# Recurrence of an RWKV-7 layer: the running sum of the log decay taken of the raw hyperbolic tangent, split in two halves

## The chip, the cores and the metric

The program runs on one core of a Trainium2 chip. The time is the device time of one execution in microseconds; the kernel before takes 2631.36 us, the median of 3 runs that lie between 2630.79 and 2633.34. TensorE does the matmuls (its weight loads are a row of their own in the profile, PEld), VectorE (DVE) and ScalarE (ACT) work on tiles, GpSimd (POOL) does a few small powers, and SyncE (SP) issues most of the DMAs. Each engine takes its instructions in order.

## The reference

The model has two layers over 256 tokens of width 2048. The first mixes tokens by RWKV-7 (32 heads of 64), the second by forgetting attention; a SwiGLU of width 5632 follows each. The change touches the decay of the RWKV-7 layer and, in passing, three small loads of the attention layer:

```python
w_log = -jax.nn.softplus(-(w0 + jnp.tanh(xw @ w1) @ w2).astype(f32)) - 0.5
decay = jnp.exp(-jnp.exp(w_log))
...
S = (S * w_t[:, :, None, :] + sa[..., None] * b_t[:, :, None, :]
     + v_t[..., None] * k_t[:, :, None, :])
```

With z for the argument of the softplus turned around, `-exp(w_log)` is `-exp(-0.5) * sigmoid(z)`, and the sigmoid is `0.5 + 0.5 * tanh(z / 2)`. So the log of the decay is `NEG_HALF_EXP * (tanh(z / 2) + 1)`, with `NEG_HALF_EXP` = -0.5 exp(-0.5).

## The kernel before

All large products run in one stream of weights (class `Stream`). Blocks of 128x512 weights come from memory as float32 and are split: ScalarE copies the block to a rounded half `wh` (L149), VectorE subtracts to get the rest `wl` (L150). Every product is then three matmuls in the fast 32-bit type, xh·wh, xh·wl and xl·wh (L175 to L177), for each of two halves of the tokens. The weights are split up to six blocks ahead of TensorE, into seven buffers.

Everything else is woven into that stream. Background work is written as generators; after each group of three stream matmuls `tick` moves every active generator to its next `yield`. So the order of the work is set by where the `yield`s stand, and then by the order in which the build lays the instructions on each engine. PSUM has four banks for the stream (`mm`) and four for the background (`bg`, taken by `take` and returned by `give`).

The recurrence of the RWKV-7 layer is computed in chunks of 64 tokens, woven into the products `r`, `w2`, `a2`, `g2` and the output projection. It has eight units: four groups g of eight heads by two halves t of the tokens. For each unit `prepare` does the following.

- It has `tw`, the log decay, 128 tokens by 512 channels, computed in the foreground after the product `w2`: a tanh on ScalarE (L938), then VectorE multiplies by and adds `NEG_HALF_EXP` (L939).
- TensorE sums `tw` over the tokens of each chunk: one float32 matmul with the triangular constant (L563) into bank `ps`. Four small ones of two columns (L565) put the sum over a whole chunk into `pc`.
- VectorE takes `ps` minus `tw` (L577); ScalarE takes exponentials of `ps`, of its negative, and of the chunk sums (L578, L579, L582), later of the difference (L591).
- Transposes (L627, L641) and copies (L635, L646) bring the scaled keys to the other layout, 16 float32 matmuls (L657) form the small matrices, and VectorE reads them out of PSUM under a mask (L660).

`solve` and `merge` invert the triangular blocks (32x32 matmuls on L734, L741, L751, L767), and `chain` carries the state from chunk to chunk (L812, L815, L821, L826, L828). `post` finishes the outputs (L859, L874, transposes on L888). A unit's matmuls on L563 and L565 are issued while the unit before is in its L657 and L767.

At the start of the attention layer the kernel loads three small vectors (`bf`, and `gains` in four pieces of 64x1) by DMAs issued on GpSimd (L1038 to L1042); VectorE scales `gains` (L1043). ScalarE issues the two DMAs of `cb` there (L1051), in between its copies of weights and the statistics of the residual (`jk`, L283).

Of the kernel before, what the change touches and what calls it, by code (L numbers as in the profile page):

```python
# [8 lines left out]
F32 = mybir.dt.float32  # L9
F32R = mybir.dt.float32r  # L10
BF16 = mybir.dt.bfloat16
AF = mybir.ActivationFunctionType
ALU = mybir.AluOpType
# [4 lines left out]
P = 128  # L18
# [4 lines left out]
N = 64  # L23
C = 64
# [4 lines left out]
NEG_HALF_EXP = -0.5 * 0.6065306597126334  # L29
# [1 line left out]
MASKED = -1.0e30  # L31
POW = 6

C_ID, C_TRI, C_IND, C_M, C_E, C_B8, C_LANE, C_I8, C_CAUSAL, C_END = 0, 128, 256, 258, 386, 450, 482, 486, 550, 678

# [4 lines left out]
def constants():  # L42
    import numpy as np

    c = np.zeros((P, C_END), np.float32)
    s = np.arange(P)
    c[:, C_ID : C_ID + P] = np.eye(P)
    c[:, C_TRI : C_TRI + P] = (s[:, None] <= s[None, :]) & (s[:, None] // C == s[None, :] // C)
    c[:, C_IND] = s < C
    c[:, C_IND + 1] = s >= C  # L50
    t = np.arange(C)
    c[:, C_M : C_M + C] = (s[:, None] % C) <= t[None, :]
    c[:, C_M + C : C_M + 2 * C] = (s[:, None] % C) < t[None, :]
    a, b = s[:, None] % 32, np.arange(32)[None, :]
    for i, m in enumerate((8, 16)):
        e = (a // (2 * m) == b // (2 * m)) & (a % (2 * m) < m) & (b % (2 * m) >= m)
        c[:, C_E + 32 * i : C_E + 32 * (i + 1)] = e
    c[:, C_B8 : C_B8 + 32] = a // 8 == b // 8
    c[:, C_LANE : C_LANE + 4] = s[:, None] % 4 == np.arange(4)[None, :]
    c[:, C_I8 : C_I8 + 64] = np.eye(8).reshape(1, 64)  # L60
    c[:, C_CAUSAL : C_CAUSAL + P] = np.where(s[None, :] <= s[:, None], 0.0, MASKED)
    return c


# [135 lines left out]
def hybrid_kernel(ctx, tc, const, x, a_norm_g, a_mix, a_w_rkv, a_w0, a_w1, a_w2, a_a0, a_a1, a_a2,  # L200
                  a_g1, a_g2, a_k_k, a_k_a, a_r_k, a_lnx_g, a_lnx_b, a_w_o, b_norm_g, b_w_in, b_b_f,
                  b_qn_g, b_kn_g, b_on_g, b_w_o, f_norm_g, f_w_gu, f_w_d, final_g, out):
    nc = tc.nc
# [34 lines left out]
    mm = nc.tensor.matmul  # L238
# [12 lines left out]
    cst = small.tile([P, C_END], F32, name="cst")  # L251
# [76 lines left out]
    with ExitStack() as actx:  # L328
# [5 lines left out]
        with ExitStack() as bctx:  # L334
# [166 lines left out]
            ps = S.gemm("k0", lhs_of(xk), ready=lambda kt: has("xk", kt))  # L501
# [14 lines left out]
            for g in range(4):  # L516
                ps = S.gemm(f"v{g}", lhs_of(xv), ready=lambda kt: has("xv", kt))
# [6 lines left out]
        with ExitStack() as bctx:  # L524
            g1 = bctx.enter_context(tc.tile_pool(name="sg", bufs=1))
# [8 lines left out]
            yF = {}  # L534
            vec, wat, rts, gts, units = {}, {}, {}, {}, {}

            def bc(v, g, name):
                t_ = g1.tile([P, 512], F32, name=name)
                nc.sync.dma_start(t_[:, :], v[g * 512 : (g + 1) * 512].partition_broadcast(P))
                return t_  # L540
# [6 lines left out]
            half = [slice(0, C), slice(C, P)]  # L547
# [6 lines left out]
            def prepare():  # L554
                for i, (g, t) in enumerate(order):
                    yield from wait(("r", g))
                    tw, ta = wat[g][0][t], wat[g][1][t]
                    vk, va, vr = vec[g][:3]
                    k = K[g][:, t, :]
                    r = rts[g][t]  # L560
                    ps = yield from S.take()
                    pc = yield from S.take()
                    mm(ps[:, :], cst[:, C_TRI : C_TRI + P], tw[:, :], start=True, stop=True)  # L563
                    for p in range(4):
                        mm(pc[:, 2 * p : 2 * p + 2], tw[:, p * P : (p + 1) * P], cst[:, C_IND : C_IND + 2], start=True, stop=True)  # L565
                    kk = u1.tile([P, 512], F32, name="kk")
# [7 lines left out]
                    W, Wp = WW[:, 0, :], WW[:, 1, :]  # L574
                    Wi = u1.tile([P, 512], F32, name="Wi")
                    wc = u3.tile([P, 8], F32, name="wc")
                    nc.vector.tensor_tensor(Wp, ps[:, :], tw[:, :], op=ALU.subtract)  # L577
                    nc.scalar.activation(W, ps[:, :], AF.Exp)  # L578
                    nc.scalar.activation(Wi[:, :], ps[:, :], AF.Exp, scale=-1.0)  # L579
                    for c in range(2):  # L580
                        for q in range(2):
                            nc.scalar.activation(wc[half[c], q:8:2], pc[half[q], c:8:2], AF.Exp)  # L582
                    S.give(2)
                    n8 = u1.tile([P, 8], F32, name="n8")
                    nc.vector.tensor_reduce(n8[:, :], h4(sq[:, :]), AX.X, ALU.add)
# [2 lines left out]
                    yield  # L588
                    yield
                    yield  # L590
                    nc.scalar.activation(Wp, Wp, AF.Exp)  # L591
                    k2 = u1.tile([P, 512], F32, name="k2")
                    nc.vector.scalar_tensor_tensor(k2[:, :], ta[:, :], -1.0, va[:, :], op0=ALU.add, op1=ALU.mult)
                    nc.vector.scalar_tensor_tensor(k2[:, :], k2[:, :], 1.0, k, op0=ALU.add, op1=ALU.mult)
# [328 lines left out]
            for g in range(4):  # L923
                ps = S.gemm(f"r{g}", lhs_of(xr), ready=lambda kt: has("xr", kt))
# [10 lines left out]
                tw = []  # L935
                for t in range(2):
                    a = g1.tile([P, 512], F32, name=f"tw{t}")
                    nc.scalar.activation(a[:, :], ps[t][:, :], AF.Tanh, scale=0.5)  # L938
                    nc.vector.tensor_scalar(a[:, :], a[:, :], NEG_HALF_EXP, NEG_HALF_EXP, op0=ALU.mult, op1=ALU.add)  # L939
                    tw.append(a)  # L940
                ps = S.gemm(f"a2{g}", lambda kt: tuple(loraw["a"]))
                ta = []
                for t in range(2):
# [85 lines left out]
    with ExitStack() as bctx:  # L1029
# [5 lines left out]
        alpha = b1.tile([P, 2, 2 * H], F32, name="alpha")  # L1035
        cq = b1.tile([P, 2, H], F32, name="cq")
        bf = b1.tile([H, 1], F32, name="bf")
        nc.gpsimd.dma_start(bf[:, :], b_b_f[0][:, None])  # L1038
        gains = b1.tile([P, 2], F32, name="gains")
        for j in range(2):  # L1040
            nc.gpsimd.dma_start(gains[j * N : j * N + N, 0:1], b_qn_g[0][:, None])
            nc.gpsimd.dma_start(gains[j * N : j * N + N, 1:2], b_kn_g[0][:, None])  # L1042
        nc.vector.tensor_scalar(gains[:, 0:1], gains[:, 0:1], N ** -0.5, None, op0=ALU.mult)  # L1043
        nc.vector.tensor_scalar(rsh[:, :], rst[:, :], 0.5, None, op0=ALU.mult)

# [324 lines left out]
```

## Time and profile before

| | |
|---|---|
| median of 3 runs | 2631.36 us |
| the profiled execution | 2630.58 us, span 2628.8 us |
| TensorE busy | 2580.2 us, 98% of the span |
| weight loads busy | 2113.8 us, 80% |
| VectorE, ScalarE busy | 1674.7 us (64%), 1481.5 us (56%) |
| mean granted clock of TensorE | 0.994 |

The profile page gives each engine's busy time, the span in 40 slices, and the chain of work that ended last. Other views used below: the waits (who waited for whom, and for how long in total, how often, and the longest), a table of stretches of the span with the busy time of each engine and the granted clock of TensorE, the timeline of single instructions (start, duration, engine, line, what it writes and reads, and in brackets the idle time before it and what ended it), and the groups of instructions by line. The units of the recurrence run from about 254 to 620 us; the attention layer begins at about 1378 us. A float32 matmul shows as two records in the timeline (x2 for one L563, x8 for four L565).

### The profile page before, as it was taken

What the parts mean: (1) busy time and instruction counts of PE and PEld (TensorE: products, weight loads), DVE (VectorE), ACT (ScalarE), POOL (GpSimd) and SP (SyncE); (2) the same over time, 40 slices, a digit from 0 to 9 for tenths busy, and PEclk for the clock granted to TensorE, in tenths of its full rate; (3) what the DMA queues carried; (4) which work ended last, traced back from release to release, by engine and by line L of the source; (5) the groups of instructions that cost most, each with busy time, mean ns of one, the idle gap of its engine ahead of it and who ended that gap; (6) DMA issues with size and microseconds to landing.
All of it is one profiled execution on the core that took longest, in us unless ns stands there. A gap on an engine that the chain in (4) does not pass through costs nothing.

```text
span 2628.8 us, 40943 instructions
## 1 busy us (share of the span) xinstructions
PE 2580.2 (98%) x15160; PEld 2113.8 (80%) x15160; DVE 1674.7 (64%) x2965; ACT 1481.5 (56%) x2869; POOL 90.0 (3%) x68
## 2 busy tenths in 40 slices
PE   7999999999999999999999999999999999999998
PEld 5788777777888888888888888888888888888886
DVE  7875887777555555555556677676755555555554
ACT  6665687776545454544455556655654545454443
POOL 0000010100000000000001010010000000000000
PEclk9999999899999999999999999999999999999999
DMA  6676323235666666655556666664566666665564
GB/s 199 184 215 208 104 87 111 88 111 156 189 190 190 187 192 185 192 192 192 190 188 203 200 201 186 184 206 153 178 191 190 189 189 191 186 192 192 197 196 153
DMA packets 253946, 468.46 MB, mean 178 GB/s; under 512 B 22249, under 2 KB 32697, under 8 KB 253745
## 3 DMA queue, kind: packets, MB, share of 16 engines
q1 hardware_dynamic: 250736, 463.62, 58.2%
q8 instruction: 119, 1.95, 0.3%
q10 hardware_dynamic: 2848, 2.22, 0.3%
q14 instruction: 83, 0.67, 0.1%
q0 software_dynamic: 160, 0.00, 0.0%
HBM read 457.37 MB, written 4.23 MB: 176 GB/s over the span
## 4 chain that ended last, share of the span: by engine, by line
PE 90%; ACT 4%; DVE 3%; DMA 1%; issue 1%; POOL 0%; SPq 0%; ACTq 0%; POOLq 0%; DVEq 0%
PE mm L175 27%; PE mm L177 27%; PE mm L176 27%; DVE wl L150 2%; ACT wh L149 1%; PE bg L989 1%; PE bg L821 1%; PE bg L657 1%; PE bg L812 1%; ACT xb L635 1%; ACT Bs L859 1%; PE bg L828 1%; PE bg L815 1%; PE bg L304 1%; DMA st<-in_a_w_rkv_dram 1%
## 5 line engine op out<-in xcount | busy, mean ns | idle before, releaser
L150 DVE TENSOR_TENSOR wl<-st,wh 128x512 fp32r<-128x512 f32 (+1 forms) x1648 | 1129.4, 690 | 812.8 <-ACT wh L149 807.4
L149 ACT CAST wh<-st 128x512 fp32r<-128x512 f32 (+1 forms) x1648 | 1015.5, 622 | 946.8 <-DVE wl L150 691.9
L175 PE MATMUL mm<-wh,xb 128*128 128x512 f32 x2048 | 803.4, 392 | 0.0
L177 PE MATMUL mm<-wh,xb 128*128 128x512 f32 x2048 | 799.8, 391 | 0.0
L176 PE MATMUL mm<-wl,xb 128*128 128x512 f32 x2048 | 799.4, 390 | 0.0
L175 PEld LDWEIGHTS mm<-wh,xb 128*128 128x128 f32 x2048 | 384.7, 188 | 79.8 <-issue 3.3
L177 PEld LDWEIGHTS mm<-wh,xb 128*128 128x128 f32 x2048 | 384.5, 188 | 79.1
L176 PEld LDWEIGHTS mm<-wl,xb 128*128 128x128 f32 x2048 | 384.8, 188 | 76.0
L176 PE MATMUL mm<-wl,xa 128*128 128x512 f32 x768 | 306.0, 398 | 3.0 <-DVE wl L150 1.6
L175 PE MATMUL mm<-wh,xa 128*128 128x512 f32 x768 | 306.9, 400 | 0.0
L177 PE MATMUL mm<-wh,xa 128*128 128x512 f32 x768 | 305.4, 398 | 0.0
L175 PE MATMUL mm<-wh,hb 128*128 128x512 f32 x448 | 174.3, 389 | 0.0
L176 PE MATMUL mm<-wl,hb 128*128 128x512 f32 x448 | 174.3, 389 | 0.0
L177 PE MATMUL mm<-wh,hb 128*128 128x512 f32 x448 | 174.3, 389 | 0.0
L176 PEld LDWEIGHTS mm<-wl,xa 128*128 128x128 f32 x768 | 145.8, 190 | 33.2 <-DVE wl L150 3.3
L177 PEld LDWEIGHTS mm<-wh,xa 128*128 128x128 f32 x768 | 145.4, 189 | 30.3 <-issue 0.2
L175 PEld LDWEIGHTS mm<-wh,xa 128*128 128x128 f32 x768 | 145.8, 190 | 29.0 <-issue 1.0
L175 PEld LDWEIGHTS mm<-wh,hb 128*128 128x128 f32 x448 | 84.1, 188 | 17.5
L176 PEld LDWEIGHTS mm<-wl,hb 128*128 128x128 f32 x448 | 84.1, 188 | 17.4
L177 PEld LDWEIGHTS mm<-wh,hb 128*128 128x128 f32 x448 | 84.1, 188 | 17.4
L1170 POOL TENSOR_TENSOR n<-n,pw 128x8 f32<-128x8 f32 x24 | 45.1, 1882 | 411.5 <-DVE n L1169 411.5
L1213 ACT ACTIVATE sc<-sc,nm 128x128 f32<-128x128 f32 x64 | 28.7, 449 | 26.6 <-DVE nm L1212 26.6
(286 smaller groups left out, 1948.2 us busy)
## 6 DMA issues: line engine op xcount, KB each, us to landing
st<-in_f_w_gu_dram SPq DMA_DIRECT2D x352, 512.0 KB
st<-in_f_w_d_dram SPq DMA_DIRECT2D x176, 512.0 KB
st<-in_b_w_in_dram SPq DMA_DIRECT2D x128, 512.0 KB
st<-in_a_w_rkv_dram SPq DMA_DIRECT2D x96, 512.0 KB
st<-in_a_w_o_dram SPq DMA_DIRECT2D x32, 512.0 KB
st<-in_b_w_o_dram SPq DMA_DIRECT2D x32, 512.0 KB
cb<-cdram SPq DMA_DIRECT2D x4, 1024.0 KB
x<-in_x_dram SPq DMA_DIRECT2D x12, 256.0 KB
```

Source lines behind the costliest of these rows:

```text
L149: nc.scalar.copy(hi[:rows, :n], st)
L150: nc.vector.tensor_tensor(lo[:rows, :n], st, hi[:rows, :n].bitcast(F32), op=ALU.subtract)
L175: nc.tensor.matmul(ps[t][:, :n], xh[:rows, c], wh, start=kt == 0, stop=False)
L176: nc.tensor.matmul(ps[t][:, :n], xh[:rows, c], wl, start=False, stop=False)
L177: nc.tensor.matmul(ps[t][:, :n], xl[:rows, c], wh, start=False, stop=kt == kts - 1)
L304: nc.tensor.transpose(tp[:, i * T + t * P : i * T + (t + 1) * P], src[:, t, c : c + P], ident)
L635: nc.scalar.copy(dst, tpv[half[q], :, c, :])
L657: mm(pm[c][:, h * P : (h + 1) * P], fkb[us, b * 4 + h, :], far[us, b * 4 + h, :], start=True, stop=True)
L812: mm(pb[us, hs], M[:, c * 8 + h, C : 2 * C], sv[:, hs], start=True, stop=True)
L815: mm(pb[vs, hs], far[us, h, 0:C], sv[us, hs], start=h == 0, stop=False)
L1170: nc.gpsimd.tensor_tensor(n8[:, :], n8[:, :], pw[:, :], op=ALU.pow)
L1213: nc.scalar.activation(sc[:, c], sc[:, c], AF.Exp, bias=nm[:, t : t + 1], accum_out=nm[:, 2 + t : 3 + t])
```

## The change

- `tw` stays the raw tanh: L939 is gone. Its factor goes into the scale of the four exponentials, and its constant, which summed over n tokens is n times `NEG_HALF_EXP`, into their bias: four new columns of the constant tile (`dec`), by token.
- In `prepare`, each unit splits `tw` into two halves of the fast 32-bit type, `th` (tile `dh`, a copy on ScalarE) and `tl` (tile `dl`, a subtraction on VectorE). The float32 matmul L563 becomes two fast ones, one for each half, with a copy `tri` of the triangular constant in that type. A `yield` is added between taking the two PSUM banks and the matmuls.
- The program sets GpSimd's DMA scratch to 1024 bytes, and the five small loads of the attention layer are issued on ScalarE instead of GpSimd.

```diff
+            tri = g1.tile([P, P], F32R, name="tri")
+            nc.vector.tensor_copy(tri[:, :], cst[:, C_TRI : C_TRI + P])
+            dec = cst[:, C_DEC : C_DEC + 4]
...
-                    tw, ta = wat[g][0][t], wat[g][1][t]
+                    (tw, th, tl), ta = wat[g][0][t], wat[g][1][t]
...
+                    nc.scalar.copy(th[:, :], tw[:, :])
+                    nc.vector.tensor_tensor(tl[:, :], tw[:, :], th[:, :].bitcast(F32), op=ALU.subtract)
                     ps = yield from S.take()
                     pc = yield from S.take()
-                    mm(ps[:, :], cst[:, C_TRI : C_TRI + P], tw[:, :], start=True, stop=True)
+                    yield
+                    mm(ps[:, :], tri[:, :], th[:, :], start=True, stop=False)
+                    mm(ps[:, :], tri[:, :], tl[:, :], start=False, stop=True)
...
-                    nc.scalar.activation(W, ps[:, :], AF.Exp)
-                    nc.scalar.activation(Wi[:, :], ps[:, :], AF.Exp, scale=-1.0)
+                    nc.scalar.activation(W, ps[:, :], AF.Exp, scale=NEG_HALF_EXP, bias=dec[:, 0:1])
+                    nc.scalar.activation(Wi[:, :], ps[:, :], AF.Exp, scale=-NEG_HALF_EXP, bias=dec[:, 1:2])
...
-                            nc.scalar.activation(wc[half[c], q:8:2], pc[half[q], c:8:2], AF.Exp)
+                            nc.scalar.activation(wc[half[c], q:8:2], pc[half[q], c:8:2], AF.Exp, scale=NEG_HALF_EXP, bias=dec[half[q], 3:4])
...
-                    nc.scalar.activation(Wp, Wp, AF.Exp)
+                    nc.scalar.activation(Wp, Wp, AF.Exp, scale=NEG_HALF_EXP, bias=dec[:, 2:3])
...
                     nc.scalar.activation(a[:, :], ps[t][:, :], AF.Tanh, scale=0.5)
-                    nc.vector.tensor_scalar(a[:, :], a[:, :], NEG_HALF_EXP, NEG_HALF_EXP, op0=ALU.mult, op1=ALU.add)
-                    tw.append(a)
+                    tw.append((a, hi, lo))
...
-        nc.gpsimd.dma_start(bf[:, :], b_b_f[0][:, None])
+        nc.scalar.dma_start(bf[:, :], b_b_f[0][:, None])
...
-            nc.gpsimd.dma_start(gains[j * N : j * N + N, 0:1], b_qn_g[0][:, None])
-            nc.gpsimd.dma_start(gains[j * N : j * N + N, 1:2], b_kn_g[0][:, None])
+            nc.scalar.dma_start(gains[j * N : j * N + N, 0:1], b_qn_g[0][:, None])
+            nc.scalar.dma_start(gains[j * N : j * N + N, 1:2], b_kn_g[0][:, None])
...
-    nc = _bacc.Bacc("TRN2", target_bir_lowering=False, num_devices=1)
+    nc = _bacc.Bacc("TRN2", target_bir_lowering=False, num_devices=1, dynamic_dma_scratch_size=1024)
```

The new lines move the line numbers: those of the stream by 3 (L175 is L178 in the changed kernel), those of `prepare` behind the split by 11 (L565 is L576, L657 is L668), those of the attention layer by 12.

The build lays the instructions of the whole recurrence anew. Three places show how.

TensorE, the matrices of the seventh unit (L657) and the running sum of the eighth. `bg` is a background bank, `mm` the stream; `xa` holds the stream's inputs. Before:

```order
L641 MATMUL bg<-cst,xb_2534 128x128 x4
L176 MATMUL mm<-wl,xa_5842 128x512
L177 MATMUL mm<-wh,xa_5843 128x512
L657 MATMUL bg<-xb_2534,WW 128x128
L175 MATMUL mm<-wh,xa_5842 128x512
L657 MATMUL bg<-xb_2534,WW 128x128 x15
L767 MATMUL bg<-Tt,Xs 32x32 x16
L563 MATMUL bg<-tw_5643,cst 128x512
L565 MATMUL bg<-cst,tw_5643 128x2 x4
L176 MATMUL mm<-wl,xa_5842 128x512
L812 MATMUL bg<-sv,xb_2535 64x64 x8
L815 MATMUL bg<-sv,xb_2535 64x64 x8
```

In the changed kernel:

```order
L762 MATMUL bg<-Ti,xb_2535 32x32 x16
L668 MATMUL bg<-xb_2534,WW 128x128 x12
L179 MATMUL mm<-wl,xa_5869 128x512
L180 MATMUL mm<-wh,xa_5870 128x512
L668 MATMUL bg<-xb_2534,WW 128x128 x4
L573 MATMUL bg<-dh_5628,tri 128x512
L574 MATMUL bg<-dl_5629,tri 128x512
L576 MATMUL bg<-cst,tw_5627 128x2 x4
L778 MATMUL bg<-Tt,Xs 32x32 x16
L178 MATMUL mm<-wh,xa_5869 128x512
L179 MATMUL mm<-wl,xa_5869 128x512
L180 MATMUL mm<-wh,xa_5870 128x512
```

The two fast matmuls stand in the place of the float32 one, and after the 32x32 matmuls six matmuls of the stream (three of them shown) come ahead of the chain's (L823 there, L812 before), where there was one.

TensorE, the end of the matrices of the fourth unit and the running sum of the fifth, before:

```order
L751 MATMUL bg<-Ti,xb_2534 32x32 x13
L657 MATMUL bg<-xb_2535,WW 128x128 x8
L563 MATMUL bg<-tw_4437,cst 128x512
L767 MATMUL bg<-Tt,Xs 32x32 x5
L565 MATMUL bg<-cst,tw_4437 128x2 x4
L767 MATMUL bg<-Tt,Xs 32x32 x11
L175 MATMUL mm<-wh,gh 128x512
```

In the changed kernel:

```order
L762 MATMUL bg<-Ti,xb_2534 32x32 x16
L668 MATMUL bg<-xb_2535,WW 128x128 x16
L573 MATMUL bg<-dh_4470,tri 128x512
L574 MATMUL bg<-dl_4471,tri 128x512
L778 MATMUL bg<-Tt,Xs 32x32 x5
L576 MATMUL bg<-cst,tw_4469 128x2 x4
L778 MATMUL bg<-Tt,Xs 32x32 x11
```

The 16 matrix products now stand together, and between the running sum and the chunk sums five 32x32 matmuls remain, as before.

ScalarE, the start of the attention layer, before:

```order
L149 CAST wh<-st 128x512 x42
L283 ACTIVATE jk_14222,ss<-x_7491 128x512
L283 ACTIVATE jk_14224,ss<-x_7491 128x512
L149 CAST wh<-st 128x512
L1051 DMA cb<-in_b_w_in_dram 128x8x96 x2
L291 ACTIVATE xb_12188<-bg,gcol 128x256
```

In the changed kernel:

```order
L152 CAST wh<-st 128x512 x40
L1050 DMA bf<-in_b_b_f_dram 32x1
L1053 DMA gains<-in_b_qn_g_dram 64x1
L286 ACTIVATE jk_14256,ss<-x_7515 128x512
L286 ACTIVATE jk_14258,ss<-x_7515 128x512
L1054 DMA gains<-in_b_kn_g_dram 64x1
L1053 DMA gains<-in_b_qn_g_dram 64x1
L1054 DMA gains<-in_b_kn_g_dram 64x1
L152 CAST wh<-st 128x512 x3
L1063 DMA cb<-in_b_w_in_dram 128x8x96 x2
```

Five small issues now stand around the two statistics, ahead of three copies of weights and the DMAs of `cb`.

More of the change, by code (lines that the diff above doesn't have):

```diff
@@ L32 @@
 POW = 6
-C_ID, C_TRI, C_IND, C_M, C_E, C_B8, C_LANE, C_I8, C_CAUSAL, C_END = 0, 128, 256, 258, 386, 450, 482, 486, 550, 678
+C_ID, C_TRI, C_IND, C_M, C_E, C_B8, C_LANE, C_I8, C_CAUSAL, C_DEC, C_END = 0, 128, 256, 258, 386, 450, 482, 486, 550, 678, 682
 A_OUT = [(0, 1, 0), (0, 2, 1), (0, 2, 2), (1, 1, 0), (0, 2, 3)] + [(2, 1, n) for n in range(4)] + [(3, 1, n) for n in range(4)]
@@ L61, in constants @@
     c[:, C_CAUSAL : C_CAUSAL + P] = np.where(s[None, :] <= s[:, None], 0.0, MASKED)
+    n = s % C + 1
+    c[:, C_DEC : C_DEC + 4] = NEG_HALF_EXP * np.stack([n, -n, n - 1, 0 * n + C], 1)
     return c
@@ L937, in hybrid_kernel @@
                     a = g1.tile([P, 512], F32, name=f"tw{t}")
+                    hi = g1.tile([P, 512], F32R, name=f"dh{t}")
+                    lo = g1.tile([P, 512], F32R, name=f"dl{t}")
                     nc.scalar.activation(a[:, :], ps[t][:, :], AF.Tanh, scale=0.5)
-                    nc.vector.tensor_scalar(a[:, :], a[:, :], NEG_HALF_EXP, NEG_HALF_EXP, op0=ALU.mult, op1=ALU.add)
-                    tw.append(a)
+                    tw.append((a, hi, lo))
                 ps = S.gemm(f"a2{g}", lambda kt: tuple(loraw["a"]))
```

## The prediction

> **What bounds the kernel now.** I read the page first, for the engines and the chain that ended last; then the granted clock, the waits of TensorE and a table of stretches, because the change lies in one stage.
>
> ```profile
> PE 2580.2 (98%) x15160; PEld 2113.8 (80%) x15160; DVE 1674.7 (64%) x2965; ACT 1481.5 (56%) x2869; POOL 90.0 (3%) x68
> PEclk9999999899999999999999999999999999999999
> PE 90%; ACT 4%; DVE 3%; DMA 1%; issue 1%; POOL 0%; SPq 0%; ACTq 0%; POOLq 0%; DVEq 0%
> ```
>
> TensorE is busy 98% of the span and makes 90% of the chain. What is taken from it in any stage shortens the run, unless it becomes a wait there. The stage of the change is the units of the recurrence:
>
> ```profile
> core 0: us, PE busy (x) PEld busy (x) DVE busy (x) ACT busy (x) POOL busy (x), PEclk, DMA share, GB/s
> 250.00:300.00 50.00, 47.47 (x371) 37.32 (x373) 44.77 (x90) 35.44 (x74) 2.31 (x2) 0.98 0.49 144
> 350.00:400.00 50.00, 47.52 (x671) 37.55 (x670) 38.71 (x92) 40.51 (x102) 5.10 (x4) 0.97 0.29 88
> 500.00:550.00 50.00, 49.54 (x655) 39.08 (x653) 36.95 (x80) 33.72 (x88) 5.04 (x4) 0.84 0.26 81
> sum 370.00, PE 355.17 PEld 280.88 DVE 291.95 ACT 279.29 POOL 34.98; mean PE 50.74 PEld 40.13 DVE 41.71 ACT 39.90 POOL 5.00
> ```
>
> The last row sums seven stretches from 250 to 620 us. TensorE is busy 355.2 of 370 us there, so 14.8 us are idle; VectorE has 78 us to spare and ScalarE 91. DMA moves at half its share or less. TensorE's idle time is many small waits:
>
> ```profile
> PE bg L641 <- ACT xb L635: 2.8, 5, 0.9
> PE bg L657 <- ACT WW L646: 2.3, 6, 0.9
> PE bg L734 <- issue: 1.8, 1, 1.8
> PE mm L176 <- issue: 1.4, 1, 1.4
> PE bg L565 <- DVE xb L660: 1.4, 1, 1.4
> ```
>
> The columns are the total, how often, and the longest. None of these is at L563: what feeds the running sum is in time today. Besides, TensorE loses time to its clock:
>
> ```profile
> 290.00:300.00 10.00, 8.21 (x174) 5.96 (x176) 9.84 (x25) 4.36 (x9) 0.36 (x1) 0.88 0.27 80
> 300.00:310.00 10.00, 8.38 (x202) 6.61 (x193) 7.31 (x13) 8.34 (x20) 1.94 (x1) 0.95 0.36 106
> 380.00:390.00 10.00, 8.63 (x96) 6.57 (x95) 8.03 (x17) 9.04 (x23) 2.01 (x1) 0.83 0.01 2
> 490.00:500.00 10.00, 9.02 (x108) 6.96 (x95) 7.93 (x15) 9.65 (x27) 1.94 (x1) 0.95 0.34 105
> 500.00:510.00 10.00, 10.00 (x86) 8.12 (x84) 8.82 (x17) 8.31 (x23) 1.94 (x1) 0.50 0.19 55
> 510.00:520.00 10.00, 10.00 (x63) 7.96 (x63) 1.50 (x5) 3.31 (x6) 0.00 (x0) 0.70 0.17 54
> ```
>
> The clock is 1.00 or 0.50. From these means, time at half clock is 2.4 + 1.0 us around 300, 3.4 at 386, and 1.0 + 10.0 + 6.0 = 17.0 us from 499 to 516: 23.8 us in all, in steps of 3.4. At half clock half the time is lost, so 11.9 us, about 1.7 for each step. [...]
>
> **The change part by part.** The float32 matmul against two fast ones, first:
>
> ```profile
> 254.49 0.39 PE L177 MATMUL mm<-wh,xa 128*128 128x512 f32 x1
> 254.72 1.02 PE L563 MATMUL bg<-tw,cst 128*128 128x512 f32 x2
> 255.57 0.95 PE L565 MATMUL bg<-cst,tw 128*128 128x2 f32 x8
> 256.38 0.49 PE L175 MATMUL mm<-wh,xa 128*128 128x512 f32 x1
> 256.71 0.40 PE L176 MATMUL mm<-wl,xa 128*128 128x512 f32 x1
> 256.94 0.40 PE L177 MATMUL mm<-wh,xa 128*128 128x512 f32 x1
> ```
>
> Durations overlap in the pipeline, so I go from start to start. L563 holds TensorE 255.57 - 254.72 = 0.85 us. A fast matmul of the same shape holds it 0.23 (256.71 to 256.94), two 0.46. That is 0.39 us less, eight times: **-3.1 us**. Where L563 falls into the half clock it holds longer,
>
> ```profile
> 502.51 2.08 PE L563 MATMUL bg<-tw,cst 128*128 128x512 f32 x2
> 504.38 1.71 PE L565 MATMUL bg<-cst,tw 128*128 128x2 f32 x8
> ```
>
> 1.87 us, against an estimate of 0.9 for the pair at that clock, which would make the sum -3.7. I take -3.1 and treat the clock by itself. Neither bound is zero: the pair has the shape and type of thousands of stream matmuls, so its price is not in doubt.
>
> Then what the saving uncovers. Right after L563 the weight load of L565 waits for VectorE to read the matrices out of the bank that `pc` takes:
>
> ```profile
> L565 PEld LDWEIGHTS bg<-cst,tw 128*128 128x128 f32 x64 | 9.1, 209 | 5.2 <-DVE xb L660 3.7 <-issue 1.4
> L660 DVE TENSOR_TENSOR xb<-bg,cst 128x512 f32<-128x512 f32 x32 | 21.3, 687 | 7.7 <-PE bg L657 7.6
> L767 PE MATMUL bg<-Tt,Xs 32*32 32x32 f32 x256 | 6.2, 198 | 0.0
> ```
>
> 3.7 us of such waiting of the weight loads, six times, lie mostly under L563 itself, because only 1.4 of it shows as a wait of TensorE above. The pair is 0.39 us shorter as a cover, so up to 6 x 0.39 = 2.3 us come back as waits, and queued behind L565 is the whole in-order stream. At the fifth unit five of the 16 L767 stand between, as before, and their share is small (6.2 us over 128 matmuls, 0.05 each, 0.25 for five); at the eighth none do. Against it, the added `yield` issues the sums three stream matmuls, 0.7 us, later, which gives VectorE that time. Bounds: 0 and +2.3; I take **+0.9**, below the middle, because of the `yield`.
>
> The split adds a copy on ScalarE and a subtraction on VectorE for each unit, and removes L939:
>
> ```profile
> L150 DVE TENSOR_TENSOR wl<-st,wh 128x512 fp32r<-128x512 f32 (+1 forms) x1648 | 1129.4, 690 | 812.8 <-ACT wh L149 807.4
> L149 ACT CAST wh<-st 128x512 fp32r<-128x512 f32 (+1 forms) x1648 | 1015.5, 622 | 946.8 <-DVE wl L150 691.9
> L939 DVE TENSOR_SCALAR tw<-tw x8: 389/419/428, 253.5 to 451.6; 128x512 f32<-128x512 f32 x8
> ```
>
> ScalarE gets 8 x 0.62 = 5.0 us, VectorE 8 x (0.69 - 0.42) = +2.2 us, within 91 and 78 us to spare, and the stream's weights are split up to six blocks ahead. The halves are made at the unit's start, far ahead of their matmuls in all units but the first of a group. **0**; if all of it lay on the chain it would be 5.0 + 2.2 = +7.2, which is a rival below. The copy `tri` (one, 128x128, less than one L150's 0.69 us) falls into the stage before 250, where VectorE waits for ScalarE more often than not. The scales and biases of the exponentials add no instruction: 0, or at most what a bias adds to 6 exponentials a unit, which no row here shows apart; L859 uses one, and it has no separate price.
>
> The loads of the attention layer move from GpSimd to ScalarE. The rows of before:
>
> ```profile
> L1041 POOL DMA_DIRECT2D gains<-in_b_qn_g_dram x2: 528/535/542, 1379.2 to 1380.2; - x2
>   DVE gains L1043: 3.8, 1
> 1379.94 0.61 ACTq L1051 DMA_DIRECT2D cb<-in_b_w_in_dram  x1
> 1387.54 0.84 ACT L291 ACTIVATE xb<-bg,gcol 128x256 fp32r<-128x256 f32 x2 [4.85 <-DVE xb L292]
> 1350.00:1700.00 350.00, 349.85 (x1714) 287.21 (x1712) 242.97 (x467) 202.13 (x397) 33.71 (x22) 1.00 0.66 196
> ```
>
> VectorE waits 3.8 us for these loads today, ScalarE behind it 4.85, and still TensorE is busy 349.85 of 350 us: the blocks split ahead cover that. Five issues of about 0.6 us on ScalarE's queue, 3 us, stand ahead of three copies and the DMAs of `cb`. If they take the place of the wait of 4.85, nothing is seen; if they add to it, the cover of six blocks (six matmuls each, 36 x 0.23 = 8.3 us) is just about used up. Bounds 0 and +3; I take **0**.
>
> The sum: -3.1 + 0.9 + 0 + 0 = -2.2 us. Against the profiled execution, 2630.58 us (1.8 outside its span, unchanged), that is 2628.4; the median of the runs lies 0.8 higher, so **2629.2 us**.
>
> **The rivals.** All of the recurrence's instructions are laid out anew, so the waits and the half clock are drawn again; that is larger than the sum.
>
> [...]
>
> [...]
>
> *The split lands on the chain.* If ScalarE and VectorE end the waits of each unit later, 7.2 us come in: 2629.2 + 7.2 = 2636.4. The waits on L635 and L646 (5.1 us together) show that TensorE does wait for ScalarE in every unit; against it, these copies come after the transposes, half a unit behind the split.
>
> *The saving is eaten whole*: the waits at L565 take 2.3 and the attention layer 1 to 3: 2630.6 to 2633.6, which reads as no change.
>
> **How the numbers follow.** A measurement of this kernel can tell about 0.2%, 5.3 us, from no change. The forecast with the eaten saving has 0.53, both within 0.2% (2626.1 to 2636.6); the stretch gone or much shorter 0.33, faster by more; the clock worse or the split on the chain 0.14, taken together as slower, though part of them would end just within. For the range I go down to 2619, which holds most of the gains between 2617.3 and 2622.4, and up to 2638, which holds one more stretch of five windows.
>
> **What would show it.** Right: two matmuls 0.23 us apart in the place of L563, the fillers behind the last unit unchanged, and no wait of TensorE at L573 or L574. The PSUM term is right if the wait of L576's weight load on L671 shows up to 2.3 us on TensorE. [...] A wait at L574 for the subtraction would mean the split is late. In the attention layer, idle time of TensorE between 1375 and 1400 us would show ScalarE's issues. I am wrong in kind if the time moves by more than 3 us outside 250 to 620 us.

## The result, and the profile after

The changed kernel takes 2651.65 us, the median of 5 runs (2641.21 to 2660.43), against 2633.34 us of the kernel before measured beside it: 1.0065 times as long, 95% interval 1.004 to 1.009. It is slower by 18 us. The forecast was 2629.2 with a range up to 2638: the change went the other way, and further than the range. In the experiments below, three executions that took far longer (3174.81 us in e11, 5241.26 in e12, 9797.82 of the kernel before beside them) count as slow and are in no ratio and no clock loss.

The profiled execution of the changed kernel took 2641.21 us (span 2639.4, clock 0.993). Its page, engines, granted clock and chain:

```profile
PE 2590.5 (98%) x15160; PEld 2117.4 (80%) x15160; DVE 1676.8 (64%) x2966; ACT 1490.2 (56%) x2877; POOL 89.8 (3%) x63
PEclk9999899899999999999999999999999999999999
PE 84%; ACT 3%; DVE 1%; issue 1%; POOL 0%; POOLq 0%; ACTq 0%; DVEq 0%
```

TensorE has as many instructions as before, and is busy 10.3 us longer. Where, a table of stretches tells; the columns are those of the prediction's tables. Before:

```profile
250.00:620.00 370.00, 355.17 (x4886) 280.88 (x4885) 291.95 (x625) 279.29 (x700) 34.98 (x25) 0.97 0.34 105
1160.00:1400.00 240.00, 239.85 (x1085) 197.48 (x1084) 133.56 (x208) 119.64 (x207) 3.50 (x6) 1.00 0.59 193
1400.00:1700.00 300.00, 300.00 (x1480) 246.44 (x1478) 213.14 (x416) 176.71 (x351) 30.21 (x16) 1.00 0.66 195
1700.00:2380.00 680.00, 680.00 (x3156) 560.58 (x3153) 412.21 (x682) 361.25 (x644) 15.59 (x9) 1.00 0.63 186
2380.00:2615.00 235.00, 235.00 (x1038) 194.62 (x1037) 122.73 (x181) 108.21 (x180) 0.00 (x0) 1.00 0.56 186
```

After:

```profile
250.00:620.00 370.00, 354.84 (x4889) 283.12 (x4888) 293.93 (x626) 288.69 (x708) 35.51 (x25) 0.96 0.35 105
1160.00:1400.00 240.00, 240.00 (x1062) 195.05 (x1061) 132.56 (x206) 117.99 (x206) 0.70 (x1) 1.00 0.58 190
1400.00:1700.00 300.00, 300.00 (x1464) 244.90 (x1463) 211.64 (x413) 175.31 (x348) 31.77 (x16) 1.00 0.66 193
1700.00:2380.00 680.00, 680.00 (x3157) 560.15 (x3156) 409.56 (x678) 360.15 (x642) 16.66 (x9) 1.00 0.63 186
2380.00:2615.00 235.00, 235.00 (x1024) 191.41 (x1023) 125.87 (x185) 109.56 (x184) 0.00 (x0) 1.00 0.57 190
```

In the stage of the change little has moved in this execution: TensorE is idle 15.2 us there, 14.8 before. Behind it TensorE hardly idles, at full clock, and still gets through fewer matmuls in the same time: 1062 for 1085, 1464 for 1480, 1024 for 1038. Those three stretches are the first down projection, the attention layer's products and the second down projection; between them, 3157 for 3156. None of their code was changed. The groups of TensorE name one kind of matmul that is slower, those that read the tile `hb` (the hidden units of the SwiGLU, read by the down projections alone). Before, then after:

```profile
L175 PE MATMUL mm<-wh,hb 128*128 128x512 f32 x448 | 174.3, 389 | 0.0
```

```profile
L178 PE MATMUL mm<-wh,hb 128*128 128x512 f32 x448 | 177.4, 396 | 0.0
```

389 became 396 ns, on this and two more lines of 448 each: 3 x (177.4 - 174.3) = 9.3 us. The matmuls on `xa` and `xb`, of the same shape, move far less: 390 to 400 ns before, 391 to 402 after.

The last transpose of the recurrence (L888, now L899) gives a second measure: where the recurrence ends, and how long the rest of the program takes. Before, then after:

```profile
L888 PE MATMUL bg<-cst,Y x32: 270/273/330, 355.3 to 615.3; 128*128 128x128 f32 x32
```

```profile
L899 PE MATMUL bg<-cst,Y x32: 272/273/474, 362.8 to 615.4; 128*128 128x128 f32 x32
```

The recurrence ends at 615.3 and 615.4 us; the rest takes 2628.8 - 615.3 = 2013.5 and 2639.4 - 615.4 = 2024.0 us. This profiled execution is the fastest of the five, though: the others spend up to 19 us more. Their granted clocks say on what. The span times one minus the mean clock goes from 18 to 40 us over the five; the span less that stays between 2618.7 and 2623.4.

### The profile page after: what moved, and what is told of

Same layout as the page of the kernel before. It is cut to its first block, busy times and chain, and to the rows that moved or that the text cites. A ratio compares the mean times of both kernels' runs of the same rounds, so it can differ in the third digit from the quotient of the medians.

```text
span 2639.4 us, 40961 instructions
## 1 busy us (share of the span) xinstructions
PE 2590.5 (98%) x15160; PEld 2117.4 (80%) x15160; DVE 1676.8 (64%) x2966; ACT 1490.2 (56%) x2877; POOL 89.8 (3%) x63
## 4 chain that ended last, share of the span: by engine, by line
PE 84%; ACT 3%; DVE 1%; issue 1%; POOL 0%; POOLq 0%; ACTq 0%; DVEq 0%
PE mm L178 26%; PE mm L180 25%; PE mm L179 25%; PE bg L1001 1%; PE bg L832 1%; ACT xb L646 1%; PE bg L668 1%; PE bg L839 1%; PE bg L307 1%; PE bg L823 1%; PE bg L837 1%; ACT Bs L870 0%; PE bg L826 0%; ACT Y L885 0%; PE bg L1234 0%
## 5 line engine op out<-in xcount | busy, mean ns | idle before, releaser
L178 PE MATMUL mm<-wh,xb 128*128 128x512 f32 x2048 | 805.8, 393 | 0.0
L178 PEld LDWEIGHTS mm<-wh,xb 128*128 128x128 f32 x2048 | 385.0, 188 | 80.5 <-issue 3.3
L178 PE MATMUL mm<-wh,xa 128*128 128x512 f32 x768 | 307.8, 402 | 0.0
L180 PE MATMUL mm<-wh,hb 128*128 128x512 f32 x448 | 177.4, 396 | 0.0
L178 PE MATMUL mm<-wh,hb 128*128 128x512 f32 x448 | 177.4, 396 | 0.0
L179 PE MATMUL mm<-wl,hb 128*128 128x512 f32 x448 | 177.4, 396 | 0.0
L178 PEld LDWEIGHTS mm<-wh,xa 128*128 128x128 f32 x768 | 144.9, 189 | 29.4 <-issue 1.2
L178 PEld LDWEIGHTS mm<-wh,hb 128*128 128x128 f32 x448 | 84.3, 188 | 20.1
```

Of the source, the lines that this page charges most:

```text
L178: nc.tensor.matmul(ps[t][:, :n], xh[:rows, c], wh, start=kt == 0, stop=False)
L179: nc.tensor.matmul(ps[t][:, :n], xh[:rows, c], wl, start=False, stop=False)
L180: nc.tensor.matmul(ps[t][:, :n], xl[:rows, c], wh, start=False, stop=kt == kts - 1)
```

## The experiments

What could have moved in untouched code is the place of the data. The four new columns make the table of constants 682 floats wide instead of 678 (2728 bytes for 2712), and every tile allocated behind it starts 32 bytes later: `hb`, and the tiles of the recurrence and of the attention layer. The smaller scratch moves every tile of the program by 15360 bytes. Seven buffers of the weight tiles `wh` and `wl`, and `xa` and `xb`, lie ahead of the table: they start 128 bytes past a multiple of 512 in both kernels. `hb` does so before (byte 161408) and no longer after (146080), and neither do two further buffers of weight tiles that the attention layer alone uses. The kernels that were timed, in one table. "Start" is the byte where `hb` starts, less that of the seven buffers of weight tiles, modulo 256. "Matmul on `hb`" is the mean duration that most of its three lines show. "Clock loss" is the span times one minus the mean granted clock, the mean over the runs; it is the time that the half clock would cost if all work there took twice as long. "End" is the last transpose of the recurrence in the profiled execution, and "rest" its span less that.

| kernel | start | matmul on `hb`, ns | median, us | ratio to before, interval | clock loss | end | rest |
|---|---|---|---|---|---|---|---|
| before (four groups of runs) | 0 | 389 | 2628.0 to 2633.1 | 1 | 13 to 16 | 615.3 | 2013.5 |
| changed | 32 | 396 | 2651.65 | 1.0065 (1.004 to 1.009) | 28 | 615.4 | 2024.0 |
| e4, changed again | 32 | 395 | 2649.50 | 1.0069 (1.0050 to 1.0088) | 27 | 620.6 | 2024.3 |
| e1, changed, 64 | 64 | 396 | 2647.91 | 1.0072 (1.0045 to 1.0099) | 28 | 622.2 | 2023.2 |
| e5, changed, 128 | 128 | 395 | 2650.09 | 1.0078 (1.0055 to 1.0101) | 31 | 626.9 | 2022.1 |
| e9, changed, 0 | 0 | 389 | 2638.18 | 1.0043 (1.0024 to 1.0061) | 29 | 625.7 | 2012.2 |
| e2, before, all behind moved | 32 | 395 | 2642.95 | 1.0041 (1.0024 to 1.0058) | 14 | 613.5 | 2025.8 |
| e3, before, scratch and loads | 0 | 389 | 2630.94 | 0.9997 (0.9982 to 1.0013) | 16 | 613.5 | 2012.1 |
| e12, before, `hb` alone | 32 | 395 | 2637.32 | 1.0032 (1.0015 to 1.0048) | 12 | 608.8 | 2022.5 |
| e13, before, `hb` alone by 256 | 0 | 389 | 2631.38 | 1.0008 (0.9992 to 1.0024) | 15 | 612.8 | 2013.9 |
| e14, before, everything by 32 | 0 | 389 | 2632.16 | 0.9999 (0.9985 to 1.0013) | 15 | 618.7 | 2012.5 |
| e15, before, everything by 384 | 0 | 389 | 2627.34 | 1.0000 (0.9983 to 1.0017) | 15 | 611.4 | 2011.8 |
| e6, no hand-back | 128 | 395 | 2641.58 | 1.0037 (1.0025 to 1.0049) | 16 | 617.6 | 2022.7 |
| e7, no split | 128 | 395 | 2638.77 | 1.0032 (1.0020 to 1.0044) | 14 | 616.0 | 2022.2 |
| e8, more matmuls | 128 | 395 | 2643.86 | 1.0045 (1.0030 to 1.0060) | 16 | 620.0 | 2022.8 |
| e10, no hand-back, 0 | 0 | 389 | 2633.00 | 1.0015 (1.0000 to 1.0029) | 16 | 618.9 | 2012.7 |
| e11, no split, 0 | 0 | 389 | 2632.34 | 1.0010 (0.9996 to 1.0024) | 15 | 615.9 | 2012.1 |
| e16, two hand-backs, 0 | 0 | 389 | 2632.74 | 1.0008 (0.9993 to 1.0022) | 16 | 622.8 | 2008.7 |

(A hand-back is a `yield`, which hands the turn back to the stream.) The rest is 2009 to 2014 us wherever `hb` starts at 0, and 2022 to 2026 wherever it doesn't, whatever the order of the recurrence. "End" compares only orders that have done as much of the stream by then: 1515 stream matmuls before, 1518 in the changed order, but 1531 in e16, so that some 3 us of e16's late end are missing in its rest. The theory was formed in steps, and its first forms fell.

**The changed kernel with its table padded.** The added columns are zeros that nothing reads, in e1, e5 and e9 alike.

```diff
-C_DEC, C_END = ..., 678, 682
+C_DEC, C_END = ..., 678, 690    (e1; 712 in e5, 808 in e9)
```

> The changed kernel with the constant tile 8 columns wider (690 instead of 682, the columns hold zeros and are not read), so that every tile allocated behind it moves by 32 bytes and starts at a multiple of 64 again, as before the change. The order of the instructions is that of the changed kernel. Theory A (address: matmuls that read their stationary operand from a tile that starts 32 bytes off a multiple of 64 go at 0.2332 us instead of 0.2267): the 1344 matmuls of hb go back from 396 to 389 ns in the rows, some 9 us are gained, and the end of the second down projection lies at most 2 us off that of before in an execution with as much half clock. Theory B (only the clock, drawn anew by the new order of the recurrence): the rows of hb stay at 396 ns and the time stays between 2641 and 2660 us. Both together: 9 us less than the changed kernel, and the spread over the runs stays.

> The changed kernel with the constant tile 712 columns wide (the last 30 hold zeros and are not read), so that hb and every tile of the later stages start at a multiple of 128 again; the order of the instructions of the recurrence is that of the changed kernel. The time of an execution is read as two parts: the time lost to the half clock (span times one minus the mean granted clock) and the rest. The rest was 2615.8 us before, 2623 for the changed kernel, 2628.4 for the kernel before with its tiles shifted. Theory A128 (a start at a multiple of 128 decides, since 32 and 64 past it were both slow): hb at 389 ns, the rest 12.6 us lower than the changed kernel's, 2610 to 2611, while the clock takes 27 us as it did: 2637 us in the middle. Theory A off (something else of the address decides): hb at 396 ns, the rest 2622 to 2623.

> The changed kernel, its table of constants padded to 808 columns with zeros that nothing reads, so that the tile hb starts at byte 146560: 128 bytes past a multiple of 512, as in the kernel before (161408) and in the run with the smaller scratch (146048), the two in which the matmul on hb took 389 ns; in the four layouts in which it took 394 to 396 ns hb started 160, 192 or 256 bytes past such a multiple. Theory (the start within 512 bytes decides, or the congruence with the weight tiles, which all start 128 bytes past one): 389 ns on hb, the time without the half clock near 2611 instead of 2623, the lost half clock as in the changed kernel (27 us), so about 2639 and a ratio near 1.003. Rival (what decides is not the start within 512 bytes, e.g. the tile's place in the memory as a whole): 395 ns, about 2650, ratio 1.007.

A start at a multiple of 64 bytes (e1) or of 128 (e5) did not bring the fast matmuls back: 396 and 395 ns, ratios 1.0072 and 1.0078. That alignment by itself matters fell with them. e9, whose `hb` lies to the weight tiles as it did before, has them:

```profile
L178 PE MATMUL mm<-wh,hb 128*128 128x512 f32 x448 | 174.3, 389 | 0.0
```

Its rest is 2012.2, as before. It is still slower than the kernel before (ratio 1.0043, some 10 us), with a clock loss of 29 us: that is the second cause, below.

**The kernel before with parts of the change.** In e2 its table is padded to 682 columns with zeros; in e3 it gets the small scratch and the loads on ScalarE. e4 is the changed kernel once more, beside them.

```diff
-..., 486, 550, 678
+..., 486, 550, 682                                       (e2)
-num_devices=1)
+num_devices=1, dynamic_dma_scratch_size=1024)            (e3, and the five loads on nc.scalar)
```

> The kernel before with the constant tile 4 columns wider (682, as in the change; they hold zeros and are not read), nothing else. The order of the instructions of the recurrence is that of before; every tile behind the constant tile starts 32 bytes further. Theory A: the rows of hb go to 396 ns, and the kernel is 9 to 12 us slower than before (2640 to 2645 us), with the spread of before. Theory B: nothing but noise, 2630 to 2636 us.

> The kernel before with two parts of the change alone: GpSimd's DMA scratch of 1024 bytes and the five small loads of the attention layer issued on ScalarE. All tiles move down by 15360 bytes, which keeps their place within 64 bytes. Theory A: no change, 2630 to 2636 us, hb at 389 ns. If the loads on ScalarE cost what the trace of the change loses between 1381 and 1850 us, 2 to 3 us more. Theory B: no change.

> The changed kernel once more, for a second profile and five more times beside the others on one chip. Theory A and B together: again a spread of 10 to 20 us, each run's time following its mean granted clock (one percent of clock is some 26 us), and a profile whose half clock lies in other units of the recurrence than in the first one; hb at 396 ns in any case.

e3 costs nothing. e2, which computes just what the kernel before computes, in the same order, takes 1.0041 times as long. That is the greater part of the loss, from four unused columns. e2 also shows the attention layer's share. Its weight tiles come from nine buffers there, two of them in a pool behind the table, so those two were moved against `xb`. The timeline of e2, TensorE:

```profile
1459.56 0.39 PE L175 MATMUL mm<-wh,xb 128*128 128x512 f32 x1
1459.79 0.39 PE L176 MATMUL mm<-wl,xb 128*128 128x512 f32 x1
1460.02 0.39 PE L177 MATMUL mm<-wh,xb 128*128 128x512 f32 x1
1460.24 0.40 PE L175 MATMUL mm<-wh,xb 128*128 128x512 f32 x1
1460.48 0.39 PE L176 MATMUL mm<-wl,xb 128*128 128x512 f32 x1
1460.71 0.40 PE L177 MATMUL mm<-wh,xb 128*128 128x512 f32 x1
...
1463.05 0.40 PE L175 MATMUL mm<-wh,xb 128*128 128x512 f32 x1
1463.29 0.39 PE L176 MATMUL mm<-wl,xb 128*128 128x512 f32 x1
1463.51 0.39 PE L177 MATMUL mm<-wh,xb 128*128 128x512 f32 x1
```

From 1460.24 to 1463.29 thirteen matmuls take 3.05 us, 0.235 each; the three ahead of them 0.68, 0.227 each. Two weight tiles serve twelve matmuls. Here `xb` had not moved and the weight tile had: the price hangs on the two operands' starts together. Over the stretch from 1400 to 1700 us TensorE gets through 1465 matmuls in e2, and through 1477 in e12, the run below in which `hb` alone moves and these two buffers stay in their place (1480 before).

**`hb` alone, and everything together.** In e12 and e13 an unused tile stands ahead of `hb` in its pool, so that only `hb` moves; in e14 and e15 one stands ahead of all tiles, so that all move alike (e15 stands on e3, for the room).

```diff
+gap = hp.tile([P, 8], F32, name="gap")        (e12: 32 bytes; e13: 64 columns, 256 bytes)
 hb = [hp.tile([P, 28, T], F32R, name=f"hb{i}") for i in range(2)]
...
+ahead = ...tile_pool(name="ahead", bufs=1)).tile([P, 8], F32, name="ahead")   (e14; 96 columns in e15)
 S = Stream(tc, ctx, plan, 4)
```

> The kernel before, with a tile of 32 bytes that nothing uses ahead of hb in its pool: hb alone starts at 161440, every other tile stays where it was. Theory (the start of hb is the cause of the greater part): 395 ns on hb, 2640 to 2643 us, ratio 1.0035 to 1.0050, against 2643 when everything behind the constants moved by 32 bytes; what is missing to 1.0041 belongs to the other tiles, those of the attention layer. Rival (the tiles that were moved with hb do it, not hb): 389 ns, 2631, ratio 1.000.

> The kernel before with an unused tile of 256 bytes ahead of hb: hb alone starts 384 bytes past a multiple of 512, 256 away from the weight tiles' start. Theory of the whole 512 bytes: 395 ns on hb, about 2638, ratio 1.003. Theory that only the start within 256 bytes counts: 389 ns, ratio 1.000. (hb at 256 past, that is at 128 away from the weight tiles, gave 394 ns.)

> The kernel before with an unused tile of 32 bytes ahead of everything: every tile of the program starts 32 bytes later (160 past a multiple of 512 where it was 128), and all of them lie to each other as before. If the start itself decides: 395 ns on hb and some 6 ns more on the matmuls on xa and xb too, of which 14,600 have the same form: over 8448 of them alone 8448 x 6.6 ns, 56 us, so 2680 or more, ratio 1.02. If the start of hb against the weight tiles decides: 389 ns, 2628 to 2631, ratio 1.000.

> The kernel before with the small scratch and its loads on ScalarE's queue, which cost nothing, and an unused tile of 384 bytes ahead of everything: every tile that lay 128 bytes past a multiple of 512 now lies at one, and all lie to each other as before. If the start itself decides, either all matmuls change (up or down, by some 6 ns of 390, over 50 us) or 0 is as good as 128 past; if the start of hb against the weight tiles decides: 389 ns, 2628 to 2631, ratio 1.000.

The groups of e12, then of e14:

```profile
L175 PE MATMUL mm<-wh,hb 128*128 128x512 f32 x448 | 177.2, 395 | 0.0
```

```profile
L175 PE MATMUL mm<-wh,hb 128*128 128x512 f32 x448 | 174.3, 389 | 0.0
```

In both `hb` starts at byte 161440. With the weight tiles left where they were the matmul is slow, with them moved along it is fast; so it is not the start itself. e13 narrows it to 256 bytes: the expectation of a whole 512 was wrong. e15 agrees. (The 56 us of the expectation for the case against were an upper figure, from all stream matmuls becoming slow.)

**Is there a better start than 0?** Two single executions of the kernel before, with unused tiles ahead of each half of `hb`, give the other distances.

```diff
+gap = hp.tile([P, ((24, 16), (48, 8))[l][i]], F32, name=f"gap{i}")      (e17)
+gap = hp.tile([P, ((40, 0 + 64), (56, 64))[l][i]], F32, name=f"gap{i}")     (e18)
```

> The kernel before with unused tiles ahead of each half of hb: against the weight tiles, modulo 256, the high half of hb starts 96 bytes past in the first down projection and 192 in the second, the low half 160 and 224. Theory (only a multiple of 256 is fast): 394 to 396 ns in both, 2637 to 2641 us, by 8 to 10 more than the kernel before. Rival (the price goes with the distance to a multiple of 64 or 128 or has a best place elsewhere): one projection at 389 ns or below, up to 2633.

> As e17, with both halves of hb 160 bytes past the weight tiles' start (modulo 256) in the first down projection and 224 in the second. Theory: 394 to 396 ns in both, 2637 to 2641 us. Rival: 389 ns or below in one of them.

2632.74 and 2635.82 us, against 2623.38 for the kernel before in the same place. On `hb` the groups by line lie between 391 and 399 ns at 96, 160, 192 and 224. None is as fast as 0.

**The second cause: the clock.** In e9 the data lie as before, and what is left of the loss is in the recurrence. Its end, in single executions, lies at 613.0 us in the mean of nine profiles of the order before (608.8 to 618.7), and at 622.2 in the mean of five of the changed order (615.4 to 626.9). The time at half clock ahead of 1350 us is 7 to 31 us in the first, 31 to 48 in the second. Starts do not do it: e2, with the tiles moved and the old order, loses 14 us to the clock, and e9, with the old start and the changed order, 29. The kernels that tell what in the order does it stand on e5:

```diff
-                    yield                                        (e6: added hand-back out)
-  copy, subtraction, two matmuls on tri
+  mm(ps[:, :], cst[:, C_TRI : C_TRI + P], tw[:, :], ...)         (e7: one float32 matmul, no halves; the yield stays)
+                    for _ in range(2):                           (e8: two more matmuls, overwritten)
+                        mm(ps[:, :], tri[:, :], th[:, :], start=True, stop=True)
```

> As e5_aligned_128 (tiles at multiples of 128), without the yield between taking the two banks and the running sum: the order is laid out anew. Theory Y (the yield made the crowded places): the clock's loss falls from 27 to the 16 us of before; with a rest near 2611 the time is 2627. Theory O (every new order draws its own loss): anything between 14 and 30 us. Theory W (float32 work kept the clock up, and taking it out lowers it): 27 us or more.

> As e5_aligned_128, with the split undone: one float32 matmul of the raw hyperbolic tangent, factor and constant still in the exponentials, the added yield kept. Theory W: the clock's loss goes back to about 16 us, because the steady float32 work is back; the rest is 3 to 5 us above that of e5. Theory Y: the loss stays at 27. Theory O: its own draw between 14 and 30 us.

> As e5_aligned_128, with two more fast matmuls per unit of the same shape ahead of the running sum, whose result is overwritten: TensorE holds 0.92 us there, as long as the float32 matmul's 0.85. Theory W: the clock's loss falls to about 16 us, and the rest rises by 8 times 0.46, 3.7 us. Theories Y and O: the loss stays at 27 or is a new draw, as the order is laid out anew.

All three bring the clock loss from 31 us back to 14 to 16, and the time down by 6 to 11 us. The float32 matmul (e7) does it, but so do the fast pair without the added `yield` (e6) and more of the fast matmuls (e8). So neither the missing float32 work nor the hand-back is the cause by itself. The last three repeat e6 and e7 with the start of e9, and add a second `yield` to e9:

```diff
+                    yield          (e16: behind the added one)
```

> As the run before it in this list, and without the added hand-back ahead of the two matmuls of the sum. Theory (start within 512 bytes, and an order that loses little to the half clock): the 2641.6 us of the kernel with the other start, less some 11: about 2630.5, clock loss 14 to 18 us, ratio 0.998 to 1.001. If the start is not what decides: 2641, ratio 1.004. If the start also moves the clock: 2639 or more at 389 ns on hb.

> The start of hb as in the kernel before, and the sum as one float32 matmul of the raw hyperbolic tangent (no halves; the hand-back, the factor and constant in the exponentials stay). Theory: the 2638.8 us of the kernel with the other start, less some 11: about 2628, clock loss 13 to 15 us, ratio 0.997 to 1.000. If the start is not what decides: 2639, ratio 1.003.

> The changed kernel with hb at the old start and a second hand-back behind the added one. If the clock loss belongs to the hand-back with the halves: 27 to 31 us lost, 2638 again, ratio 1.004. If it belongs to the one order that happened to come out: 13 to 17 us lost, 2628 to 2633, ratio 1.000 to 1.002.

e16 has both the hand-back and the halves, and its clock loss is 16 us, as before the change. The stretches around the two places where e9 loses most, first e9, then e16:

```profile
310.00:320.00 10.00, 9.10 (x73) 6.84 (x74) 5.76 (x10) 8.50 (x20) 0.00 (x0) 0.61 0.18 60
320.00:330.00 10.00, 10.00 (x70) 8.29 (x70) 5.80 (x17) 5.00 (x13) 0.00 (x0) 0.54 0.04 13
480.00:490.00 10.00, 10.00 (x90) 8.90 (x90) 5.62 (x20) 5.93 (x14) 0.00 (x0) 0.69 0.13 42
510.00:520.00 10.00, 10.00 (x65) 8.24 (x63) 7.89 (x16) 7.97 (x21) 1.94 (x1) 0.50 0.28 80
```

```profile
310.00:320.00 10.00, 9.55 (x186) 7.87 (x185) 6.93 (x12) 8.70 (x20) 0.00 (x0) 0.88 0.16 55
320.00:330.00 10.00, 10.00 (x109) 8.57 (x108) 6.32 (x17) 8.26 (x19) 0.00 (x0) 1.00 0.05 15
480.00:490.00 10.00, 9.52 (x74) 7.71 (x74) 7.26 (x26) 6.55 (x15) 0.90 (x1) 0.68 0.28 84
510.00:520.00 10.00, 10.00 (x104) 7.72 (x101) 8.47 (x16) 9.79 (x23) 0.00 (x0) 1.00 0.08 13
```

The clock column is the third from the end. e16 keeps it where e9 has 0.54 and 0.50. So the loss belongs to this one order, and one more hand-back in it takes the loss away. What in the order starts a half-clock stretch stays open: idle time of TensorE ahead of it doesn't tell the two apart (from 300 to 310 us TensorE is busy 7.17 us in e9 and 6.63 in e16).

The clock loss fell by 15 to 18 us from e5 to e6, e7 and e8, and the time by 6 to 11 only. In e8 the added matmuls make 8 x 0.46 = 3.7 us of the difference; two more things lie between. Among executions of one kernel a microsecond of clock loss goes with some 0.8 us of span (0.83 over 282 executions of 21 groups), so the column is somewhat too large as a price. (In the profile of before a matmul of the stream takes 0.43 us from start to start at half clock, from 511 to 515 us, and 0.23 at full: 1.9 times as long, not twice.) And but for the clock the changed order is the shorter one: e9 has 15.6 us more clock loss than the kernel before in the same group, 13 us at that rate, but its mean span is only 9.6 us longer (2637.2 against 2627.6), so by this estimate some 3 us are gained elsewhere.

No version beats the kernel before by more than its interval; e10, e11 and e16 equal it or lie 2 to 4 us above.

## Why the prediction was wrong

**Where the 18 us are.** Some 8 to 11 lie in the rest of the program, by the starts (2024.0 against 2013.5 in the two profiles; e12 costs 0.32%, 8 us, and e2 0.41%, 11 us). Some 5 to 9 lie in the recurrence (mean ends 622.2 against 613.0; by the medians e5 against e6 8.5 us, e9 against e10 5.2). That second share is a net one. By the estimate of 0.83 us for each us of clock loss, the clock takes 8 to 14 us more in e1, e4, e5 and e9 than in the kernel before of their groups, and the order gives back some 3.

**The step that failed** is the sum's boundary: it priced instructions, waits and queues, and took everything outside the recurrence as unchanged but for the loads. That the constants get four more columns was known; no term asked what lies behind that table, and there 8 to 11 us were lost. The prediction named the sign of this error, a move of more than 3 us outside 250 to 620 us, but gave it no chance. A second step failed with it: the sum left the half clock at what it was in one execution, 23.8 us, although the prediction itself says that it is drawn again, and the draw cost 8 to 14 us by that estimate. What the sum did price came out near its -2.2: the 3 us that the changed order gives back. That these come from the pair is likely by their size, and not shown by themselves.

**The pair in place of the float32 matmul, -3.1.** Its price was right. The second unit of the changed kernel in the timeline:

```profile
280.60 0.39 PE L573 MATMUL bg<-dh,tri 128*128 128x512 f32 x1
280.83 0.40 PE L574 MATMUL bg<-dl,tri 128*128 128x512 f32 x1
281.06 0.95 PE L576 MATMUL bg<-cst,tw 128*128 128x2 f32 x8
```

0.23 us apart, 0.46 in all. But the kernels that hold the pair at the old start and keep the clock, e10 and e16, gain nothing by it: their ratios are 1.0015 and 1.0008, where -2.2 us would be 0.9992, below both intervals. The one without the split, e11, has 1.0010. The stage from 250 to 620 us, e10 and then e16, to hold against the row of before above:

```profile
250.00:620.00 370.00, 350.40 (x4880) 278.12 (x4879) 293.48 (x619) 286.93 (x704) 37.94 (x25) 0.97 0.34 104
250.00:620.00 370.00, 347.97 (x4881) 277.09 (x4881) 292.08 (x618) 286.51 (x703) 34.05 (x25) 0.98 0.34 105
```

TensorE is idle 19.6 and 22.0 us there, against 14.8 before. One wait of the chain for ScalarE makes 5.0 us in e10 (L831 waits for the copy on L828). So in these orders waits of other parts took what the pair saves; the rival "eaten whole" was right about them, though not about the place. (Its lower end, 2630.6, leaves out the 1 us of the attention layer that it names; with it the end is 2631.6.)

**The wait for the bank, +0.9,** had the wrong sign in the changed order. Waits of the changed kernel's TensorE, with the columns of the prediction's:

```profile
PE bg L762 <- ACT xb L646: 1.7, 4, 0.5
PE bg L652 <- ACT xb L646: 1.6, 4, 0.7
PE bg L668 <- ACT WW L657: 1.4, 3, 0.6
PE bg L576 <- DVE xb L671: 0.5, 1, 0.5
PE bg L573 <- ACT dh L568: 0.4, 1, 0.4
```

The wait on L671 went down from 1.4 to 0.5 (0.9 in e1, e4 and e5), so the cover that the shorter pair took away was not missed. Without the added `yield`, in e6 and e10, it is 2.1, which has the sign of the term and agrees with the prediction's argument that the `yield` works against it.

**The split at 0** held: L573 waits for the copy once, 0.4 us, where the prediction said no wait. The waits for ScalarE's copies, 2.8 and 2.3 before, are 1.6 and 1.4, with 1.7 more on L762; together 4.7 for 5.1. The rival of the split on the chain fell.

**The moved loads at 0** held, by e3 and by the stretch where they would show:

```profile
1375.00:1400.00 25.00, 25.00 (x121) 20.54 (x120) 18.09 (x35) 14.79 (x29) 0.70 (x1) 1.00 0.74 220
```

**The clock rivals.** The prediction said that the half clock is drawn anew, and put 0.33 on less of it and at most 0.14 on more. More came. No run shows what begins or ends a stretch at half clock, so none shows the terms that set the range: the gains that lead to 2622.4 and 2617.3, and one more stretch of five windows (five steps of 3.4 us, 17.0 in all, of which half, 8.5, would be lost). What the runs showed in their place is a draw: 41 to 48 us at half clock ahead of 1350 us in e1, e4, e5 and e9 and 31 in the profiled execution of the changed kernel, against 7 to 31 in the order of before, at a cost of 8 to 14 us by the estimate above. That 8.5 lies in there is in part luck. Theory W of the experiments, that float32 work keeps the clock up, fell: e6, e8 and e16 have no float32 sum and lose 16 us to the clock, for 13 to 16 in the kernel before.

## What to carry to other kernels

A change that makes a tile longer moves every tile behind it (in e2 four unused columns moved them by 32 bytes and cost 0.41%): compare the start addresses before and after, and the mean duration of untouched matmuls of one shape. Where the stationary and the moving operand of a stream were a multiple of 256 bytes apart, pad so that they stay so (here 389 ns for a matmul at such a distance, 391 to 399 at the others). An order that comes out of `yield`s is one draw of the clock; one more `yield` is a cheap second draw (clock loss 29 us in e9, 16 with one more in e16), and should be tried before the change itself is judged.

## What the runs showed of the hardware

A matmul of the fast 32-bit type, 128x512 behind its own weight load, takes 389 ns in the profile (0.227 us from start to start on `hb` in the kernel before, and in the fast rows of e2) where the starts of its two operands are a multiple of 256 bytes apart in their partitions, and 391 to 399 at 32, 64, 96, 128, 160, 192 and 224 bytes apart (from start to start, at 32: 0.233 us on `hb` in the changed kernel and in e2, 0.235 on `xb` in the slow rows of e2). The two operands are the one that the weight load puts into the array, here `hb` or `xb`, and the one that is streamed through it, here a weight tile of the model. Both move together without effect (389 ns in e14 and e15). The mean weight load on `hb` is 188 ns in the kernel before, in the changed kernel and in e5. So 3 to 3.5% from start to start hang on the distance of the two starts (0.233 to 0.235 against 0.227 us, at 32 bytes). Which part of the chip meets there is not shown.
